# Two residuals taken one token tile at a time, and two matrix units whose last four weight chunks go token by token

## The chip, the cores and the metric

The kernel runs on one core of a Trainium2 chip. The metric is the device time of one execution in microseconds (us); lower is better. A core has five engines that run side by side, each through its own queue in order: PE (TensorE, matrix products and transposes), ACT (ScalarE), DVE (VectorE), POOL (GpSimd) and SP (here the issuer of most DMAs). Results of PE land in PSUM, from which ACT and DVE read.

## The reference, cut to what matters

The program is one layer of a hybrid decoder trunk: three token mixers, a merge, an MLP and a gated per-layer embedding, on 256 tokens of width 2048, in float32. The change touches the end of the mixer, the end of the MLP, and what follows each:

```python
mixed = jnp.sum(gates * up, axis=2) @ w_out[i]
x = x + rmsnorm(mixed, post_mix_norm[i])
h = rmsnorm(x, pre_mlp_norm[i])
m = jnp.square(jax.nn.relu(h @ w_up[i])) @ w_down[i]
x = x + rmsnorm(m, post_mlp_norm[i])
ple_gate = jax.nn.sigmoid(rmsnorm(x, ple_pre_norm[i]) @ w_ple_gate[i])
e = (p[i] @ w_ple_proj[i]) * ple_gate
x = x + rmsnorm(e, ple_post_norm[i])
```

`w_out` is 2048 x 2048, `w_up` 2048 x 8192, `w_down` 8192 x 2048, `w_ple_gate` 2048 x 2048, `w_ple_proj` 256 x 2048. The root mean square of a token runs over all 2048 columns, so a token's scale is known only when its last column block is.

## The kernel before

**Tiles.** The 256 tokens are two token tiles t = 0 and 1 of 128 partitions; the 2048 columns are four column blocks cb of 512, or 16 blocks k of 128. For the next product x must stand transposed (columns on partitions), as a pair hi and lo of rounded value and rest, `ahi` and `alo`, of 16 x 256 elements per partition (one buffer each).

**Weights.** `weights` (L289) brings a chunk of 2 x 128 rows by 512 columns: SP's DMA into `raw` (4 buffers), ACT's cast into `hi` (L302, 4 buffers), DVE's rest into `lo` (L303, recorded at L170, 4 buffers). A buffer comes free when PE has used its chunk, and the cast of the chunk four later waits for that.

**Products.** `gemm_tok` (L306) makes one unit of 512 columns for both token tiles: for each chunk 12 matmuls of 512 columns, three for each of two k and two tokens. In the last chunk (`held=1`) token 0's matmuls go ahead of token 1's; the rule is `elif kc + CK > nkt - held * CK: continue`, which gathers the steps of the last `held` chunks before they are sorted by token. The last unit of `w_ple_gate` already has `held=4`. `gemm_feat` (L333), used for `w_up`, has weights as the stationary side and both tokens side by side (256 columns), 24 matmuls for each chunk; so its first matmul needs k = 0 of both tokens.

**Seam 1**, between `w_out` and `w_up`: the last `w_out` unit's evac takes the sum of squares (`square_sum`, L1116, ACT, into `ssp`) and the product with the gain (`mx`, DVE). PE goes on with one small unit `proj_unit(0)` (12 matmuls of `w_ple_proj`; ACT copies it to `pj`). Meanwhile `residual` (L1146) makes the scale of both tokens at once (`rstd_of`, L1118: sum, scale, ACT square root L258, reciprocal L260, three small DVE steps), then, column block by column block, adds to x (`xr[t]`, called `b` in the trace; L1154, recorded at L173), transposes (PE, L123, into `br`, 4 banks) and splits (ACT L180 into `ahi`, DVE L173 into `alo`, 256 columns at a time). `stats` then squares the new x for the next norm, in ACT's free time.

**Seam 2**, between `w_down` and `w_ple_gate`, is the same with three `proj_unit`s (36 matmuls) behind the last `w_down` unit, and `gemm_tok` behind it, which takes the two tokens in turn, k by k. DVE also forms eight products `pg<-pj,b` there.

**Order.** A scheduler writes a fixed order for each engine, by priorities and its own costs; `residual` and the evacs stand under `tc.high_priority()`.

Of the kernel before, what the change touches and what calls it, by code (L numbers as in the profile page):

```python
# [12 lines left out]
ALU = mybir.AluOpType  # L13
AX = mybir.AxisListType

P = 128
# [36 lines left out]
def tile_hybrid_block(ctx: ExitStack, tc: tile.TileContext, *args):  # L53
# [118 lines left out]
    def stt(o, i0, s, i1, op0, op1):  # L172
        V.scalar_tensor_tensor(out=o, in0=i0, scalar=s, in1=i1, op0=op0, op1=op1)  # L173
# [132 lines left out]
    def gemm_tok(parts, act, nkt, evac, k0=0, held=1):  # L306


        n = sum(p[2] for p in parts)
        pb = [mbank() for _ in range(NT)]  # L310
        steps = []
        for kc in range(0, nkt, CK):
            hl = weights(parts, k0 + kc, CK, OFF_TOK)
            steps += [(kc, k, t, hl) for k in range(CK) for t in range(NT)]
            if kc + CK == nkt:
                steps.sort(key=lambda p: p[2])
            elif kc + CK > nkt - held * CK:
                continue
            for i, (kc_, k, t, (hi, lo)) in enumerate(steps):
                kt = kc_ + k  # L320
                xh, xl = act(kt, t)
                o = pb[t][:, :n]
                PE.matmul(o, lhsT=xh, rhs=hi[:, k, :n], start=(kt == 0), stop=False)
                PE.matmul(o, lhsT=xh, rhs=lo[:, k, :n], start=False, stop=False)
                PE.matmul(o, lhsT=xl, rhs=hi[:, k, :n], start=False, stop=(kt == nkt - 1))
                if i % 2:
                    background()
                if kt == nkt - 1:
                    with tc.high_priority():
                        evac(t, pb[t][:, :n])  # L330
            steps = []
# [786 lines left out]
    def rstd_of(parts):  # L1118
        n = parts.shape[1]
        s = sm(n)  # L1120
        V.tensor_reduce(out=s, in_=parts, axis=AX.X, op=ALU.add)
        return rstd(s, n, 1.0 / D)
# [10 lines left out]
    for cb in range(4):  # L1133
        def evac(t, pb, cb=cb):
            if cb == 0 and t == 0:
                phase_b()
            if t == 0:
                mg.append([tb("mx") for _ in range(NT)])
            if cb == 0:
                A.sqrt(out=sm(1), in_=r0[:, :1])  # L1140
            square_sum(pb, 512, ssp[:, t, cb:cb + 1])
            tt(V, mg[cb][t], pb, gains["g1"][:, cb * 512:(cb + 1) * 512], ALU.mult)
        gemm_tok([(w_out, cb * 512, 512)], macts, KT, evac)
    proj_unit(0)

    def residual(mg, parts, gcol):  # L1146

        hi, lo = actpair()
        with tc.high_priority():
            r = rstd_of(parts)  # L1150
            for cb in range(4):
                for t in range(NT):
                    xs = xr[t][:, cb * 512:(cb + 1) * 512]
                    stt(xs, mg[cb][t], r[:, t:t + 1], xs, ALU.mult, ALU.add)  # L1154
                for k in (0, 2):
                    transpose_into(lambda kt, t: xr[t][:, kt * P:(kt + 1) * P], (cb * 4 + k, cb * 4 + k + 1),
                                   hi, lo, cb * 4 + k, lambda kt: gainT[:, gcol + kt:gcol + kt + 1])
        out_r = const.tile([P, NT], F32, name=nm("rn"))

        def stats():  # L1160
            for t in range(NT):
                for cb in range(4):
                    square_sum(xr[t][:, cb * 512:(cb + 1) * 512], 512, ssn[:, t, cb:cb + 1])
                yield 1.0
            V.tensor_copy(out=out_r, in_=rstd_of(ssn))
        return acts(hi, lo), out_r, spawn(stats(), 6.0)
# [15 lines left out]
    for s in range(NSLAB):  # L1182
        hh = [mlp[0].tile([P, SK, S], F32R, tag=f"m{i}", bufs=1, name=nm(f"m{i}_")) for i in range(2)]
        for u in range(SLAB // 512):
            def evac(b, pb, u=u, hh=hh):
                z = t2()
                stt(r3(z, S), pb, 0.0, r2bc.unsqueeze(1).broadcast_to([P, 2, S]), ALU.max, ALU.mult)
                z2 = t2()
                tt(V, z2, z, z, ALU.mult)
                k = u * 4 + 2 * b  # L1190
                split_from(r3(z2, S), hh[0][:, k:k + 2, :], hh[1][:, k:k + 2, :])
            gemm_feat([(w_up, s * SLAB + u * 512, 512)], xact, KT, evac)
        mact = acts(*hh)
        for cb in range(4):
            def evac(t, pb, cb=cb, s=s):
                if s == 0:
                    A.copy(out=macc[cb][t], in_=pb)
                else:
                    tt(V, macc[cb][t], macc[cb][t], pb, ALU.add)
                if s == NSLAB - 1:  # L1200
                    square_sum(macc[cb][t], 512, ssp[:, t, cb:cb + 1])
                    tt(V, macc[cb][t], macc[cb][t], g3[:, cb * 512:(cb + 1) * 512], ALU.mult)
            gemm_tok([(w_down, cb * 512, 512)], mact, SK, evac, k0=s * SK)
    for cb in range(1, 4):
        proj_unit(cb)
    xact, r4, _ = residual(macc, ssp, 16)
# [67 lines left out]
```

## Time and profile before

| | |
|---|---|
| median of three runs | 1872.37 us (1867.6 to 1876.28) |
| the profiled execution | 1868.37 us |
| its span, first to last instruction | 1866.6 us |
| PE busy | 1829.7 us (98%) |
| DVE, ACT, POOL busy | 1160.5, 935.9, 184.2 us |
| mean granted TensorE clock | 0.992 |

The profile is one execution. All times below are us from the start of its span. A row of the timeline gives start, length, engine, line, operation, output and inputs, count, and in brackets the idle time of the engine before it with what ended it. Lengths overlap: a matmul of 512 columns lasts 0.39 us and the next starts about 0.227 us after it, so what a queue spends on an instruction is read from start to start.

### The profile page before, as it was taken

The page shows a single profiled execution, that of the slowest core. Times are in us where ns is not written, and L with a number is a line of the kernel's source. Part 1 is how long each engine was busy: PE and PEld are TensorE (multiplying, and loading weights), DVE is VectorE, ACT ScalarE, POOL GpSimd, SP SyncE. Part 2 cuts the span into 40 slices and gives each one's busy share as a digit, 9 for nine tenths or more (in the row PEclk, how much of TensorE's full clock was granted, in tenths as well). Part 3 has the DMA queues.
Part 4 walks back from the last instruction along what each step waited for, and adds up shares of the span by engine and source line. Part 5 has one row for each costly group of instructions (what it writes and reads, how often), then busy time and mean ns, then how long its engine had stood idle before and what let it go on. Part 6 is the DMA issues. An engine that isn't in the chain of part 4 may idle for free.

```text
span 1866.6 us, 28343 instructions
## 1 busy us (share of the span) xinstructions
PE 1829.7 (98%) x11256; PEld 1640.7 (88%) x11256; DVE 1160.5 (62%) x1518; ACT 935.9 (50%) x1200; POOL 184.2 (10%) x243
## 2 busy tenths in 40 slices
PE   8999999899999999999999999999999999999997
PEld 7999989899888788888888898899889988998886
DVE  6567847878567666554565765455555654565675
ACT  6745555576464565444444644444433433444654
POOL 0003814800201220000000000000000000000001
PEclk9999989999999999999999999999999999999999
DMA  7766556465665546666676566666666656666563
GB/s 251 217 188 181 143 165 190 125 191 145 205 203 169 170 139 193 196 184 192 191 243 204 187 194 193 193 192 183 192 193 189 188 195 193 183 190 192 180 211 128
DMA packets 185573, 348.07 MB, mean 186 GB/s; under 512 B 14296, under 2 KB 33103, under 8 KB 184544
## 3 DMA queue, kind: packets, MB, share of 16 engines
q1 hardware_dynamic: 182992, 334.69, 59.3%
q0 software_dynamic: 2416, 11.56, 1.9%
q8 instruction: 88, 1.44, 0.3%
q14 instruction: 45, 0.37, 0.1%
q10 hardware_dynamic: 32, 0.01, 0.0%
HBM read 340.41 MB, written 5.80 MB: 185 GB/s over the span
## 4 chain that ended last, share of the span: by engine, by line
PE 69%; ACT 1%; POOL 1%; DVE 1%; issue 0%; DVEq 0%; ACTq 0%
PE mm L114 67%; POOL b L170 1%; PE br L114 1%; PE br L123 1%; ACT hi L302 0%; DVE lo L170 0%; DVE b L173 0%; ACT b L947 0%; ACT b L948 0%; ACT L1228 0%; ACT b L1116 0%; ACT L1238 0%; ACT b L1226 0%; DVE s L173 0%; ACT b L941 0%
## 5 line engine op out<-in xcount | busy, mean ns | idle before, releaser
L170 DVE TENSOR_TENSOR lo<-raw,hi 128x1024 fp32r<-128x1024 f32 (+2 forms) x644 | 773.7, 1204 | 610.4 <-ACT hi L302 608.9
L302 ACT CAST hi<-raw 128x1024 fp32r<-128x1024 f32 (+2 forms) x644 | 654.1, 1019 | 793.2 <-PE mm L114 694.6
L114 PE MATMUL mm<-ahi,hi 128*128 128x256 f32 x1728 | 485.4, 281 | 0.0
L114 PE MATMUL mm<-alo,hi 128*128 128x256 f32 x1728 | 484.6, 281 | 0.7 <-DVE alo L173 0.7
L114 PE MATMUL mm<-ahi,lo 128*128 128x256 f32 x1728 | 484.5, 280 | 0.0
L114 PE MATMUL mm<-lo,ahi 128*128 128x512 f32 (+2 forms) x992 | 370.1, 373 | 3.2 <-DVE lo L170 2.1
L114 PE MATMUL mm<-hi,ahi 128*128 128x512 f32 (+2 forms) x992 | 372.9, 376 | 0.0
L114 PE MATMUL mm<-hi,alo 128*128 128x512 f32 (+2 forms) x992 | 368.4, 371 | 0.0
L114 PEld LDWEIGHTS mm<-ahi,lo 128*128 128x128 f32 x1728 | 329.0, 190 | 0.1
L114 PEld LDWEIGHTS mm<-alo,hi 128*128 128x128 f32 x1728 | 326.1, 189 | 1.7 <-DVE alo L173 0.9
L114 PEld LDWEIGHTS mm<-ahi,hi 128*128 128x128 f32 x1728 | 326.4, 189 | 0.6 <-ACT ahi L180 0.2
L114 PE MATMUL mm<-hi,m 128*128 128x512 f32 x1024 | 316.0, 389 | 0.0
L114 PEld LDWEIGHTS mm<-hi,m 128*128 128x128 f32 x1024 | 192.2, 188 | 39.8
L114 PEld LDWEIGHTS mm<-lo,ahi 128*128 128x128 f32 x992 | 187.7, 189 | 32.8 <-DVE lo L170 4.2
L114 PEld LDWEIGHTS mm<-hi,ahi 128*128 128x128 f32 x992 | 187.6, 189 | 28.2 <-issue 0.2
L114 PEld LDWEIGHTS mm<-hi,alo 128*128 128x128 f32 x992 | 187.7, 189 | 27.5
L114 PE MATMUL mm<-lo,m 128*128 128x512 f32 x512 | 199.3, 389 | 0.0
L114 PE MATMUL mm<-hi,b 128*128 128x512 f32 x416 | 134.1, 394 | 0.7 <-ACT hi L302 0.7
L114 PEld LDWEIGHTS mm<-lo,m 128*128 128x128 f32 x512 | 96.1, 188 | 19.8
L170 POOL TENSOR_TENSOR b<-b 128x128 f32<-128x128 f32 (+16 forms) x118 | 77.7, 673 | 160.1 <-ACT b L941 147.5
L114 PEld LDWEIGHTS mm<-hi,b 128*128 128x128 f32 x416 | 78.1, 188 | 17.0 <-ACT hi L302 1.1
L114 PE MATMUL mm<-lo,b 128*128 128x512 f32 x208 | 81.3, 391 | 0.8 <-DVE lo L170 0.8
(257 smaller groups left out, 1127.1 us busy)
## 6 DMA issues: line engine op xcount, KB each, us to landing
raw<-in_w_in_dram SPq DMA_DIRECT2D x200, 512.0 KB, 3.7
raw<-in_w_up_dram SPq DMA_DIRECT2D x128, 512.0 KB, 3.7
raw<-in_w_down_dram SPq DMA_DIRECT2D x128, 512.0 KB, 3.9
raw<-in_w_branch_dram SPq DMA_DIRECT2D x48, 512.0 KB, 4.5
raw<-in_w_in_dram SPq DMA_DIRECT2D x48, 344.0 KB, 3.6
raw<-in_w_out_dram SPq DMA_DIRECT2D x32, 512.0 KB, 4.9
raw<-in_w_ple_gate_dram SPq DMA_DIRECT2D x32, 512.0 KB, 4.7
raw<-in_w_in_dram SPq DMA_DIRECT2D x16, 352.0 KB, 3.2
```

The costliest lines, as they stand in the source:

```text
L114: nc.tensor.matmul(o, lhsT=lhsT, rhs=rhs, start=start, stop=stop, **kw)
L123: nc.tensor.transpose(o, i, ident)
L170: eng.tensor_tensor(out=o, in0=i0, in1=i1, op=op)
L302: A.copy(out=hi[:, :, :n], in_=raw[:, :, :n])
```

## The change

`residual` runs its outer loop over the two token tiles: each has its own scale (`rstd_of` on one column of sums), then for each column block the add, four transposes of 128 columns of that token into one bank, and four splits of 128 columns (where two tokens were split together, 256 columns). The last units of `w_out` and of `w_down` (fourth slab) get `held=4`: their last four chunks go first for token 0 (24 matmuls), then for token 1 (24).

```diff
-        gemm_tok([(w_out, cb * 512, 512)], macts, KT, evac)
+        gemm_tok([(w_out, cb * 512, 512)], macts, KT, evac, held=4 if cb == 3 else 1)
     proj_unit(0)
 
     def residual(mg, parts, gcol):
 
         hi, lo = actpair()
         with tc.high_priority():
-            r = rstd_of(parts)
-            for cb in range(4):
-                for t in range(NT):
+            for t in range(NT):
+                r = rstd_of(parts[:, t:t + 1, :])
+                sl = slice(t * P, (t + 1) * P)
+                for cb in range(4):
                     xs = xr[t][:, cb * 512:(cb + 1) * 512]
-                    stt(xs, mg[cb][t], r[:, t:t + 1], xs, ALU.mult, ALU.add)
-                for k in (0, 2):
-                    transpose_into(lambda kt, t: xr[t][:, kt * P:(kt + 1) * P], (cb * 4 + k, cb * 4 + k + 1),
-                                   hi, lo, cb * 4 + k, lambda kt: gainT[:, gcol + kt:gcol + kt + 1])
+                    stt(xs, mg[cb][t], r, xs, ALU.mult, ALU.add)
+                    pt = bank()
+                    for i in range(4):
+                        PE.transpose(pt[:, i * P:(i + 1) * P], xs[:, i * P:(i + 1) * P], ident)
+                    for i in range(4):
+                        k = cb * 4 + i
+                        split_from(pt[:, i * P:(i + 1) * P], hi[:, k, sl], lo[:, k, sl], gainT[:, gcol + k:gcol + k + 1])
...
-            gemm_tok([(w_down, cb * 512, 512)], mact, SK, evac, k0=s * SK)
+            gemm_tok([(w_down, cb * 512, 512)], mact, SK, evac, k0=s * SK,
+                     held=4 if s == NSLAB - 1 and cb == 3 else 1)
```

Instructions: ACT has 34 more (16 splits and one square root at each seam), DVE 44 more (16 splits and six steps of the scale at each seam); the transposes stay 32 at each seam, and SP's and POOL's orders are the same as before.

**Place 1: PE in seam 1.** Before; `b_1617`, `b_1618` are the operand of `w_ple_proj`, `b_1620` and `b_1621` are x of token 0 and 1, `cst` is the identity, `mm_10061` the first bank of `w_up`:

```order
L114 MATMUL mm_9931<-lo_9934,b_1617_9433 128x512
L114 MATMUL mm_9931<-hi_9933,b_1618_9434 128x512
L123 MATMUL br_9969<-cst,b_1620_9437 128x128
L123 MATMUL br_9978<-cst,b_1620_9437 128x128
L123 MATMUL br_9969<-cst,b_1621_9439 128x128
...
L123 MATMUL br_9989<-cst,b_1620_9437 128x128
L123 MATMUL br_9998<-cst,b_1620_9437 128x128
L114 MATMUL mm_10061<-ahi_9952,hi_10064 128x256
L114 MATMUL mm_10061<-ahi_9952,lo_10065 128x256
```

Of the change (`mm_10106` is now the first bank of `w_up`):

```order
L114 MATMUL mm_9931<-lo_9934,b_1617_9433 128x512
L123 MATMUL br_9968<-cst,b_1620_9437 128x128 x4
L114 MATMUL mm_9931<-hi_9933,b_1618_9434 128x512
L123 MATMUL br_9982<-cst,b_1620_9437 128x128 x4
L123 MATMUL br_9996<-cst,b_1620_9437 128x128 x4
L123 MATMUL br_10010<-cst,b_1620_9437 128x128 x4
L123 MATMUL br_10037<-cst,b_1621_9439 128x128 x4
L123 MATMUL br_10051<-cst,b_1621_9439 128x128 x4
L123 MATMUL br_10065<-cst,b_1621_9439 128x128 x4
L123 MATMUL br_10079<-cst,b_1621_9439 128x128 x4
L114 MATMUL mm_10106<-ahi_9952,hi_10109 128x256
```

Before, the first matmul of `w_up` stood behind ten transposes; now it stands behind all 32, the last 16 of which are of token 1.

**Place 2: DVE and ACT in seam 1.** DVE before, from the step that follows the last chunk's evac (`s_...` are the small steps of the scale, `mx_...` the products with the gain):

```order
L256 TENSOR_SCALAR s_1729_9956<-s_1728_9954 128x2
L170 TENSOR_TENSOR lo_10125<-raw_10123,hi_10124 128x1024
L260 RECIPROCAL s_1731_9960<-s_1730_9958 128x2
L170 TENSOR_TENSOR s_1732_9962<-s_1731_9960 128x2
L173 SCALAR_TENSOR_TENSOR s_1732_9962<-s_1732_9962,s_1729_9956 128x2
L173 SCALAR_TENSOR_TENSOR s_1733_9965<-s_1732_9962,s_1731_9960 128x2
L173 SCALAR_TENSOR_TENSOR b_1620_9437<-mx_9441,s_1733_9965,b_1620_9437 128x512
L173 SCALAR_TENSOR_TENSOR b_1621_9439<-mx_9442,s_1733_9965,b_1621_9439 128x512
```

DVE of the change, at the scale of token 0:

```order
L256 TENSOR_SCALAR s_1729_9956<-s_1728_9954 128x1
L170 TENSOR_TENSOR lo_9934<-raw_9932,hi_9933 128x1024
L260 RECIPROCAL s_1731_9960<-s_1730_9958 128x1
L170 TENSOR_TENSOR s_1732_9962<-s_1731_9960 128x1
L170 TENSOR_TENSOR lo_10110<-raw_10108,hi_10109 128x1024
L173 SCALAR_TENSOR_TENSOR s_1732_9962<-s_1732_9962,s_1729_9956 128x1
L173 SCALAR_TENSOR_TENSOR s_1733_9965<-s_1732_9962,s_1731_9960 128x1
L170 TENSOR_TENSOR lo_10140<-raw_10138,hi_10139 128x1024
L170 TENSOR_TENSOR mx_9897<-mm_9775,b_1619_9435 128x512
L173 SCALAR_TENSOR_TENSOR b_1620_9437<-mx_9441,s_1733_9965,b_1620_9437 128x512
```

ACT of the change, at the scale of token 1 (`s_1740`; the splits of token 0 above it begin with `br_9968` and go on in the same way, 16 in all):

```order
L1116 ACTIVATE b_1773_10190,ssn<-b_1620_9437 128x512
L180 ACTIVATE ahi_9952<-br_9968,rowT_493 128x128
L180 ACTIVATE ahi_9952<-br_9982,rowT_493 128x128
L180 ACTIVATE ahi_9952<-br_9996,rowT_493 128x128
L180 ACTIVATE ahi_9952<-br_10010,rowT_493 128x128
...
L258 ACTIVATE s_1740_10027<-s_1739_10025 128x1
L1116 ACTIVATE b_1774_10192,ssn<-b_1620_9437 128x512
L1116 ACTIVATE b_1775_10206,ssn<-b_1621_9439 128x512
L1116 ACTIVATE b_1776_10208,ssn<-b_1621_9439 128x512
L180 ACTIVATE ahi_9952<-br_10037,rowT_493 128x128
```

The adds of token 0 stand behind three weight rests and behind token 1's product `mx_9897`; the square root of token 1 stands behind all 16 splits of token 0.

**Place 3: PE and DVE in seam 2.** PE of the change, where token 1's transposes begin (`mm_16824` and `mm_16825` are the banks of the first `w_ple_gate` unit for token 0 and 1):

```order
L114 MATMUL mm_16824<-hi_16897,ahi_16678 128x512
L114 MATMUL mm_16824<-lo_16898,ahi_16678 128x512
L114 MATMUL mm_16824<-hi_16897,alo_16679 128x512
L123 MATMUL br_16763<-cst,b_1621_9439 128x128 x4
L123 MATMUL br_16777<-cst,b_1621_9439 128x128 x4
L114 MATMUL mm_16825<-hi_16827,ahi_16678 128x512
L123 MATMUL br_16791<-cst,b_1621_9439 128x128 x4
```

Before, the transposes of both tokens begin inside the last small unit (`mm_16612`) and end among the first `w_ple_gate` matmuls:

```order
L114 MATMUL mm_16612<-hi_16614,b_1617_9433 128x512
L123 MATMUL br_16650<-cst,b_1620_9437 128x128
L123 MATMUL br_16659<-cst,b_1620_9437 128x128
L114 MATMUL mm_16612<-lo_16615,b_1617_9433 128x512
L114 MATMUL mm_16612<-hi_16614,b_1618_9434 128x512
L123 MATMUL br_16650<-cst,b_1621_9439 128x128
```

DVE of the change, ahead of token 1's first add there:

```order
L260 RECIPROCAL s_2723_16755<-s_2722_16753 128x1
L170 TENSOR_TENSOR lo_16898<-raw_16896,hi_16897 128x1024
L173 SCALAR_TENSOR_TENSOR alo_16679<-br_16722,rowT_493,ahi_16678 128x128
L173 SCALAR_TENSOR_TENSOR alo_16679<-br_16736,rowT_493,ahi_16678 128x128
L170 TENSOR_TENSOR s_2724_16757<-s_2723_16755 128x1
L170 TENSOR_TENSOR pg<-pj_9928,b_2731_16819 128x512
...
L170 TENSOR_TENSOR pg<-pj_9929,b_2731_16819 128x512
L173 SCALAR_TENSOR_TENSOR s_2725_16760<-s_2724_16757,s_2723_16755 128x1
L170 TENSOR_TENSOR pg<-pj_16606,b_2731_16819 128x512
L173 SCALAR_TENSOR_TENSOR b_1621_9439<-mx_10097,s_2725_16760,b_1621_9439 128x512
```

Before, both tokens were through the scale together, ahead of any `pg` product; now token 1's scale is spread between weight rests, splits and `pg` products, and on PE its transposes follow 24 matmuls of token 0.

## Rows read from the trace of the kernel before

**Rows 1.** The page: busy time of the engines, share of the span, instructions.
```profile
PE 1829.7 (98%) x11256; PEld 1640.7 (88%) x11256; DVE 1160.5 (62%) x1518; ACT 935.9 (50%) x1200; POOL 184.2 (10%) x243
```
**Rows 2.** Timeline of PE around seam 1.
```profile
1038.66 0.39 PE L114 MATMUL mm<-hi,alo 128*128 128x512 f32 x1
1041.38 0.39 PE L114 MATMUL mm<-hi,b 128*128 128x512 f32 x1
1043.47 0.44 PE L123 MATMUL br<-cst,b 128*128 128x128 f32 x2 [1.70 <-DVE b L173]
1044.13 1.10 PE L123 MATMUL br<-cst,b 128*128 128x128 f32 x8 [0.22 <-DVE b L173]
1045.24 0.39 PE L114 MATMUL mm<-ahi,hi 128*128 128x256 f32 x1
...
1062.72 0.68 PE L114 MATMUL br<-cst,rb 128*128 128x128 f32 x4 [0.39 <-DVE rb L408]
1063.16 0.37 PE L114 MATMUL mm<-alo,hi 128*128 128x256 f32 x1
```
**Rows 3.** The chain that ended last, in order of time, in seam 1.
```profile
1053.47 5.59 PE mm L114 x49
1063.40 699.54 PE mm L114 x4514
```
**Rows 4.** Timeline of DVE in seam 1.
```profile
1042.27 0.36 DVE L173 SCALAR_TENSOR_TENSOR s<-s,s 128x2 f32<-128x2 f32 x2
1042.66 2.74 DVE L173 SCALAR_TENSOR_TENSOR b<-mx,s,b 128x512 f32<-128x512 f32 x4
1045.32 0.87 DVE L173 SCALAR_TENSOR_TENSOR alo<-br,rowT,ahi 128x256 fp32r<-128x256 f32 x2
...
1052.99 1.22 DVE L170 TENSOR_TENSOR lo<-raw,hi 128x1024 fp32r<-128x1024 f32 x1
```
**Rows 5.** Timeline of ACT in seam 1.
```profile
1039.67 1.04 ACT L302 CAST hi<-raw 128x1024 fp32r<-128x1024 f32 x1
1040.61 0.59 ACT L1111 COPY pj<-mm 128x512 f32<-128x512 f32 x1
...
1046.06 1.56 ACT L180 ACTIVATE ahi<-br,rowT 128x256 fp32r<-128x256 f32 x4
1047.48 0.66 ACT L1116 ACTIVATE b<-b 128x512 f32<-128x512 f32 x1
...
1052.30 0.64 ACT L1116 ACTIVATE b<-b 128x512 f32<-128x512 f32 x1
...
1052.91 0.64 ACT L1116 ACTIVATE b<-b 128x512 f32<-128x512 f32 x1
```
**Rows 6.** Groups by form: 128 columns from PSUM on ACT and DVE (busy us, mean ns).
```profile
L941 ACT COPY b<-br 128x128 f32<-128x128 f32 x8 | 2.0, 252 | 0.0
L170 DVE TENSOR_TENSOR cbm<-br,cst 128x128 f32<-128x128 f32 x4 | 1.1, 286 | 1.9 <-PE br L114 1.9
```
**Rows 7.** The timeline of PE: its longest idle stretch.
```profile
342.98 1.11 PE L123 MATMUL br<-cst,b 128*128 128x128 f32 x4 [6.04 <-ACT b L459]
```
**Rows 8.** Windows: length, busy PE, PEld, DVE, ACT, POOL (instructions), granted clock, DMA share, GB/s.
```profile
340.00:341.00 1.00, 0.00 (x0) 0.00 (x0) 1.00 (x2) 0.00 (x0) 0.92 (x2) 0.72 0.41 54
343.00:346.00 3.00, 3.00 (x14) 3.00 (x15) 1.89 (x5) 0.85 (x2) 2.77 (x4) 0.50 0.43 116
347.00:348.00 1.00, 1.00 (x10) 1.00 (x9) 0.83 (x1) 0.14 (x1) 0.92 (x2) 0.87 0.00 0
1041.50:1045.00 3.50, 1.58 (x12) 1.04 (x10) 3.36 (x9) 2.54 (x5) 0.00 (x0) 1.00 0.88 301
```
**Rows 9.** Timelines in seam 2: PE, and ACT behind the first unit.
```profile
1755.53 0.39 PE L114 MATMUL mm<-hi,m 128*128 128x512 f32 x1
...
1762.98 0.44 PE L123 MATMUL br<-cst,b 128*128 128x128 f32 x2
...
1790.36 1.06 ACT L302 CAST hi<-raw 128x1024 fp32r<-128x1024 f32 x1 [1.66 <-PE mm L114]
```

## The prediction, made before the changed kernel was run

> **What bounds the kernel now.** I read the page first. PE is busy 98% of the span, the next engine, DVE, 62% [rows 1]: nearly everything hides behind PE, and time is won or lost only where PE stands still. Next I read PE's timeline at the two seams that the change rewrites. In seam 1 PE ends the small unit with the matmul at 1041.38, then stands 1.70 and 0.22 us before transposes and 0.39 us before the row broadcast: 2.31 us in all [rows 2]. In seam 2, with 36 small matmuls as cover instead of 12, the transposes start at 1762.98 right behind the matmuls, and nothing is idle to speak of [rows 9]. In the chain of waits one unbroken stretch of PE, 699.54 us long, follows seam 1 [rows 3]: what seam 1 loses or gains is carried to the end. So the change can win some 2.3 us at most. What it can lose is as long as the new order makes PE wait, and that has to be followed queue by queue.
>
> **Prices, from start to start.** A 512-column matmul takes (1041.38 - 1038.66)/12 = 0.227 us [rows 2], a 256-column one 5.59/49 = 0.114 [rows 3]. DVE: a 512-column add 2.66/4 = 0.665, a 256-column split (0.87 - 0.08)/2 = 0.395, a weight rest 1.22 - 0.08 = 1.14 (the last 0.08 of each overlap the next, as the add shows: 0.74 for the last of four that take 2.66 from start to start), a small step 0.39/2 = 0.19 [rows 4]. ACT: a cast 0.94, a copy `pj` 0.49 (0.59 long, less the cast's overlap of 0.10), a 256-column split 1.42/4 = 0.355, a square with its read 0.61 [rows 5]. A group of four transposes takes about 0.46 (eight take 1.10 to the end of the last) [rows 2].
>
> The new 128-column split does not occur. It cannot cost less than half of the wide one (0.18 on ACT, 0.20 on DVE) nor more than the whole (0.355, 0.395), since each pair of new splits does one old one's columns. The nearest rows are 128 columns from PSUM at 252 ns on ACT and 286 ns on DVE [rows 6]; against the 512-column copy's 0.59 us [rows 5] that is about 0.9 ns for a column on ACT, and against the add's 0.74 us about 1.2 ns on DVE. So I take off 128 columns at 0.9 and 1.0 ns: 0.25 on ACT, 0.26 on DVE. A gain is excluded here: the columns are the same and the instructions twice as many. The Trainium skill (page "ScalarE: Activation LUTs", section "What ACT_TABLE_LOAD costs") gives an ACTIVATE 186 ns + 0.833 ns a column, 93 ns more for a pointer operand, 93 ns of overlap: an estimate of 0.29 us for 128 columns. By that page the seam 1 sum below would be some 0.4 us longer; for 256 columns it would say 0.40, where this trace shows 0.355, so the trace's slope stands.
>
> **Held chunks, alone.** The same 48 matmuls run in another order. The fourth held chunk's cast waits for the chunk before the four, as now, and is ready some 2.4 us into token 0's pass, where its first matmul comes 18 x 0.227 = 4.1 us in: no wait. The cost is later: held buffers come free only during token 1's pass, after its 6th, 12th, 18th and 24th matmul.
>
> **Seam 1, step by step, on the clock of the trace of before.** The last `w_out` matmul starts at 1038.66 as before [rows 2], so token 0 is finished 24 matmuls earlier, at 1038.66 + 0.39 - 5.44 = 1033.6.
>
> *Head start of token 0.* Its sum of squares and square root could be through by about 1036.2. But on DVE three weight rests and token 1's product stand between (place 2). Their casts wait for the buffers freed at 1035.0, 1036.3 and 1037.7; each is followed by 1.14 us on DVE, with the small steps in between: the rests start at 1036.1, 1037.6 and 1039.1, token 1's product at 1040.3, and the first add of token 0 at 1040.9, the fourth at 1042.9 (end 1043.6). Before, the first add was at 1042.66 [rows 4]. A head start of 5.4 us has become 1.8.
>
> *PE.* The small unit hides the adds up to 1041.4; the four groups of token 0 follow the adds and end at 1044.1. Next in PE's queue is token 1's first group, and no matmul of `w_up` stands ahead of it (place 1).
>
> *Scale of token 1.* Its square root is queued on ACT behind all of token 0's splits (place 2). ACT first squares token 0's two new blocks as their adds end (1041.6, 1042.3) and is through the second `pj` copy at 1043.4; then 16 splits x 0.25 + a cast 0.94 + a square 0.61 = 5.55: the root at about 1049.0. DVE, with a weight rest first and then the lo splits at 0.26 behind ACT's, is through at 1049.55. Then reciprocal 0.19, one more weight rest 1.14, three small steps 0.57: the first add of token 1 at 1051.45, its end at 1052.2. PE stands from 1044.1 to 1052.26: 8.1 us, where before it stood 1.9.
>
> *The clock.* PE's one idle stretch of this length in the trace is 6.04 us, from 336.94 to 342.98 [rows 7]. The granted clock was at its upper level (2.4 GHz) until some way into 340 to 341 (mean 0.72, so until 340.4), at its lower (0.50, 1.2 GHz) from 343 to 346, and up again in 347 to 348 (mean 0.87, so from 347.3), 4.3 us after PE took up work [rows 8]. The 1.70 us stand in seam 1 left it at 1.00 [rows 8]. So here the clock is down when token 1's groups come, and each takes 2 x 0.46: 1052.26 + 3.7 = 1055.95. If it is up again 4.3 us after 1052.26, the first 0.6 us of `w_up` runs at half pace (0.3 lost). Splits of token 1 keep ahead of `w_up` from there: k = 0 is split by 1054.6, k = 3 by 1057.7, and 24 matmuls of a chunk take 2.74.
>
> *Sum.* Before, 125 matmuls of `w_up` and the row broadcast (0.44 from 1062.72) were done when the matmul at 1063.16 started, with 22 of the transposes between them [rows 2]. Now: 1055.95 + 0.3 + 125 x 0.114 + 0.44 = 1070.9. Loss **+7.8 us**. Were the clock to hold, the groups would end at 1054.7 and the loss would be +6.2. Were it up again only 4.3 us after `w_up` begins, 2.1 instead of 0.3 would be lost there: +9.6. Splits at their upper bound add 1.6, at their lower bound take off 0.7 (ACT's root is then not the last to come; DVE's rests are).
>
> **Seam 2.** 36 small matmuls cover more. The last `w_down` matmul starts at 1755.53 [rows 9], so the held buffers come free at 1751.8, 1753.2 and 1754.6; three casts and rests bring DVE to 1757.2, token 1's sum to 1757.8, and token 0's adds start at 1757.8, 1758.4, 1760.0 and 1761.1, with a product and splits between. PE waits only 0.3 for the first group. PE then has the rest of the small units and 24 matmuls of `w_ple_gate` for token 0 and comes to token 1's transposes at 1771.5 (place 3). ACT has one copy, two squares, three splits' worth and a cast until 1761.5, then ten splits, four copies, a square and a cast up to token 1's root: 10 x 0.25 + 4 x 0.49 + 0.61 + 0.94 = 6.0, root at 1767.5. DVE reaches the reciprocal at 1768.6, behind two weight rests; then a rest 1.14, three splits 0.78, three `pg` products (priced as the add, 0.665) and small steps that tuck in at 0.08: first add at 1772.9, end 1773.6. PE waits 2.1. Later it meets matmuls of the fifth `w_ple_gate` chunk, whose cast stands behind 11 splits and three squares on ACT (cast at 1777.7) and whose rest ends at 1780.0: waits of 0.9 and 0.5. By the end of the unit's 96 matmuls (before: 1790.3, the release that the cast at 1790.36 waited for [rows 9]) I get 1793.9. Loss **+3.6 us**. This is the softer number: every wait is short against the sums it comes from; I bound it by 1.0 (the first and last waits gone, the middle one halved) and 5.5 (each sum 10% longer).
>
> **Total.** +7.8 + 3.6 = +11.4 us. Against the profiled execution: 1868.37 + 11.4 = 1879.8 (span 1878.0, and 1.8 around it). That execution lay 4.0 below the median of the three runs, so for a median I predict 1872.37 + 11.4 = **1883.8 us**. A measurement of this kernel can tell about 0.5% from no change, that is 9.4 us: the forecast is slower by 0.6%, only just outside.
>
> **Rivals.**
> *Small loss, no measurable change* (chance 0.28): seam 1 as above with the clock held (+6.2), and seam 2 near its lower bound (+1.0 to +3): +7.2 to +9.2, 1880 to 1881.5. For it: seam 2 has the long cover, and in seam 1 the transposes resume little by little. Against it: PE stands longer than in the stretch where the clock did fall.
> *Larger loss* (0.13): the clock comes back late in seam 1 (+9.6) and falls in seam 2 as well, where PE stands 2.1 us and soon twice more (about +2 on 3.6): +15.2, 1887.6. For it: the return after 4.3 us is a single observation, and PE resumes here in four pieces that wait for DVE. Against it: the stand of 1.70 left the clock alone.
> *The head start works* (0.04), the other side: token 0's adds, transposes and splits run under token 1's pass, only token 1's path remains, and PE's 2.31 us of idle in seam 1 go: 1870.1. Place: DVE's queue. It decides for this if the adds of token 0 start before about 1036.5, so that their 16 splits end with token 1's matmuls; they would start at 1040.9, since three weight rests stand ahead and wait for buffers that the held chunks keep. I find nothing for it in the orders.
> That the change doesn't do what it says is excluded by the orders shown.
>
> **How the numbers follow.** Forecast (+9.4 to +13.5) 0.55, small loss 0.28, larger 0.13, head start 0.04. The range takes in the small and the larger loss (+7.2 to +15.2) and 3.5 us on either side, since medians of three move too (the three runs span 8.7): low 1872.37 + 3.7 = 1876, high 1872.37 + 18.7 = 1891; it leaves out the head start. Slower by over 0.5%: most of the forecast, all of the larger loss, 0.65; within 0.5%: the small loss and the forecast's edge, 0.33; faster 0.02.
>
> **What would show it.** Right: PE's wait for DVE's adds at L173 (now 1.9 us, 2 times) grows to about 8 in seam 1 and 2 more in seam 2; the granted clock falls to 0.5 for some 8 us near 1048 and is back before 1060; the square root of token 1 in seam 1 lies some 5.5 us behind ACT's first narrow split; narrow splits on ACT come 0.25 apart. Wrong: `w_up` begins before 1050 (the head start works, or the narrow splits are far cheaper); the clock stays at 1.00 (then +9.9 in all); seam 2 shows no wait at its second token (then about +8).

## The result, and the profile after

The changed kernel takes 1883.21 us (median; 1881.14 to 1887.27) against 1868.52 us of before, run beside it: a ratio of 1.0068, 95% interval 1.0048 to 1.0088, slower by 0.7%. The prediction was 1883.8 us and slower. The medians lie 14.7 us apart, the ratio stands for 12.7, and the five executions of before span 8.7, so it is in part luck that the forecast of the median was met within 0.6 us. The profiled execution of the changed kernel took 1881.42 us, with a span of 1879.6 us, 13.0 us more than that of before.

The sum came out, the parts less so. To see them, every trace is read in the same way: the start of a matmul is counted from the start of the last `w_out` matmul (1038.66 in [rows 2], 1038.62 after), so that what differs ahead of the change drops out. Three marks on PE then cut the difference from before: PE's 183rd instruction after that matmul (needless ones of the experiments not counted; for e7 twelve more, which it moves ahead; it lies behind the row broadcast in all traces but e9's), at the end of `w_up`'s first slab, and at the last matmul of all.

| | seam 1, to the 183rd instruction | rest of the first `w_up` slab | later `w_up` slabs | seam 2 | sum |
|---|---|---|---|---|---|
| predicted | +7.8 | 0 | 0 | +3.6 | +11.4 |
| measured | +6.5 | +2.8 | 0.0 | +3.2 | +12.6 |

PE's timeline in seam 1, the changed kernel; it answers to [rows 2]:

```profile
1041.41 0.66 PE L123 MATMUL br<-cst,b 128*128 128x128 f32 x4
1042.14 1.98 PE L123 MATMUL br<-cst,b 128*128 128x128 f32 x12
1051.83 3.29 PE L123 MATMUL br<-cst,b 128*128 128x128 f32 x16 [7.71 <-DVE b L173]
1054.88 0.37 PE L114 MATMUL mm<-ahi,hi 128*128 128x256 f32 x1
...
1065.86 0.61 PE L114 MATMUL br<-cst,rb 128*128 128x128 f32 x4
```

Where PE stood 1.70 and 0.22 us, it now stands 7.71 (the total below takes in seam 2's 1.78). The row broadcast no longer waits. PE's waits, the whole span (total, times, longest):

```profile
PE br L123 <- DVE b L173: 9.5, 2, 7.7
```

What PE waits for stands on ACT and DVE. ACT in seam 1, from token 0's second half on (it answers to [rows 5]):

```profile
1046.11 0.68 ACT L1116 ACTIVATE b<-b 128x512 f32<-128x512 f32 x1
1046.63 0.26 ACT L1116 ACTIVATION_READ_ACCUMULATOR b<-b 128x1 f32 x1
1046.72 2.22 ACT L180 ACTIVATE ahi<-br,rowT 128x128 fp32r<-128x128 f32 x8
1048.71 0.32 ACT L258 ACTIVATE s<-s 128x1 f32<-128x1 f32 x1
```

Token 1's square root is the last row: it came when the sixteenth split of token 0 was done, 10.1 us after the last `w_out` matmul (before: 2.4). DVE beside it (answers to [rows 4]):

```profile
1038.88 1.23 DVE L170 TENSOR_TENSOR lo<-raw,hi 128x1024 fp32r<-128x1024 f32 x1
1040.02 0.68 DVE L170 TENSOR_TENSOR mx<-mm,b 128x512 f32<-128x512 f32 x1
1040.62 2.73 DVE L173 SCALAR_TENSOR_TENSOR b<-mx,s,b 128x512 f32<-128x512 f32 x4
...
1044.47 2.19 DVE L173 SCALAR_TENSOR_TENSOR alo<-br,rowT,ahi 128x128 fp32r<-128x128 f32 x8
...
1047.17 2.16 DVE L173 SCALAR_TENSOR_TENSOR alo<-br,rowT,ahi 128x128 fp32r<-128x128 f32 x8 [0.45 <-ACT ahi L180]
1049.25 0.15 DVE L260 RECIPROCAL s<-s 128x1 f32<-128x1 f32 x1
1049.32 1.21 DVE L170 TENSOR_TENSOR lo<-raw,hi 128x1024 fp32r<-128x1024 f32 x1
...
1051.02 2.74 DVE L173 SCALAR_TENSOR_TENSOR b<-mx,s,b 128x512 f32<-128x512 f32 x4
```

Token 0's adds start at 1040.62, right behind the third weight rest and token 1's product; token 1's adds at 1051.02, behind all splits of token 0, a reciprocal, another rest and the small steps. The granted clock of the same stretch (windows; columns: width, busy time of PE, PEld, DVE, ACT and POOL with counts, clock, DMA share, GB/s; answers to [rows 8]):

```profile
1046.00:1047.00 1.00, 0.00 (x0) 0.00 (x0) 0.72 (x4) 1.00 (x6) 0.00 (x0) 1.00 0.92 360
1047.00:1048.00 1.00, 0.00 (x0) 0.00 (x0) 0.83 (x4) 1.00 (x6) 0.00 (x0) 0.89 0.85 336
1048.00:1051.00 3.00, 0.00 (x0) 0.00 (x0) 2.92 (x11) 1.64 (x7) 0.00 (x0) 0.50 0.14 55
1051.00:1054.00 3.00, 2.17 (x10) 2.17 (x11) 2.98 (x5) 2.19 (x7) 0.00 (x0) 0.50 0.58 175
1054.00:1055.00 1.00, 1.00 (x9) 1.00 (x8) 0.62 (x3) 1.00 (x5) 0.00 (x0) 0.70 0.00 0
1055.00:1060.00 5.00, 5.00 (x47) 5.00 (x46) 4.52 (x18) 4.63 (x17) 0.00 (x0) 1.00 0.01 3
```

It fell at about 1047.8 and was back at about 1054.6, some 2.8 us after PE took up work. PE in seam 2 (answers to [rows 9], which has no idle time):

```profile
1782.61 1.32 PE L123 MATMUL br<-cst,b 128*128 128x128 f32 x8 [1.78 <-DVE b L173]
...
1787.69 0.77 PE L114 MATMUL mm<-hi,ahi 128*128 128x512 f32 x2 [0.57 <-ACT hi L302]
1788.95 0.50 PE L114 MATMUL mm<-lo,ahi 128*128 128x512 f32 x1 [0.25 <-DVE lo L170]
```

**A term that was not in the sum.** PE does not wait in the rest of the first `w_up` slab, neither before nor after, and yet the changed kernel loses 2.8 us there. One of PE's three groups of `w_up` matmuls from 1080 to 1120, before (count; busy time, mean ns of one; idle time):

```profile
L114 PE MATMUL mm<-ahi,lo 128*128 128x256 f32 x119 | 32.9, 276 | 0.0
```

The same group in the changed kernel:

```profile
L114 PE MATMUL mm<-ahi,lo 128*128 128x256 f32 x114 | 32.1, 281 | 0.0
```

With the other two groups that is 355 matmuls before and 342 after in the same 40 us, the two or three that only reach into the window counted in. From start to start it is one every 0.1133 or every 0.1178 us (the pace; 272 or 283 cycles at the granted 2.4 GHz). Over some 630 matmuls of the slab that makes 2.8 us. In the changed kernel the matmuls run at 0.1133 up to the row broadcast and at 0.1178 from there to the end of the slab. Slabs 2 to 4 run at 0.1178 in both kernels.

### The profile page after: what moved, and what is told of

It is laid out like the page before. It is cut to its first block, busy times and chain, and to the rows that moved or that the text cites. A ratio compares the mean times of both kernels' runs of the same rounds, so it can differ in the third digit from the quotient of the medians.

```text
span 1879.6 us, 28418 instructions
## 1 busy us (share of the span) xinstructions
PE 1835.1 (98%) x11256; PEld 1645.5 (88%) x11256; DVE 1167.2 (62%) x1562; ACT 940.3 (50%) x1234; POOL 183.0 (10%) x243
## 4 chain that ended last, share of the span: by engine, by line
PE 68%; ACT 2%; DVE 1%; POOL 1%; issue 1%; DVEq 0%; ACTq 0%
PE mm L114 66%; POOL b L170 1%; PE br L114 1%; PE br L123 1%; ACT hi L302 1%; DVE lo L170 1%; ACT b L1116 0%; ACT ahi L180 0%; DVE b L173 0%; ACT pj L1111 0%; ACT b L947 0%; ACT b L948 0%; DVE alo L173 0%; DVE pg L170 0%; DVE pj L170 0%
```

## The experiments

The theory from the prediction, S: the order inside the new residual costs, above all the root of token 1 behind token 0's splits. The rival, H: the held chunks cost, since they bring three weight rests ahead of the adds. Later ones are told where they came up. Differences below are of the traces, from the last `w_out` matmul; ratios are of times, against before beside it. Each kernel has one trace. How far such a difference repeats is seen where the order of seam 1 is the same: the order of the changed kernel stands in e3 and e12 as well, and the three lose 6.5, 6.9 and 6.7 us there; the order of before stands in e11 and e6 as well, which lose 0.0 and, with a fall of the clock (see e9), 1.3.

**e1: held chunks alone.**

```diff
-        gemm_tok([(w_out, cb * 512, 512)], macts, KT, evac)
+        gemm_tok([(w_out, cb * 512, 512)], macts, KT, evac, held=4 if cb == 3 else 1)
...
-            gemm_tok([(w_down, cb * 512, 512)], mact, SK, evac, k0=s * SK)
+            gemm_tok([(w_down, cb * 512, 512)], mact, SK, evac, k0=s * SK,
+                     held=4 if s == NSLAB - 1 and cb == 3 else 1)
```

> Only the held chunks of the change (both units), with the residual of before, both tokens' scale at once. Theory S (the order inside the new residual costs: token 1's square root stands on ACT behind token 0's sixteen splits): the seams stay within 2 us of before, because nothing new stands ahead of the roots; 1868 to 1871 us, ratio 1.000 to 1.002, PE's wait at the adds stays near 2 us and the granted clock stays at 1.00 there. Rival H (the held chunks cost: they keep weight buffers, so three weight rests come late and stand on DVE ahead of the adds): most of the loss is here already, 1876 us or more.

Ratio 1.0007 (0.9992 to 1.0021). Seam 1 -0.07 us, all else 0.00: the three rests do come late, but they end just as token 1's sum is due. H falls.

**e2: the new residual alone** (the diff of the change without the two `held` lines).

> Only the new residual, one token tile at a time, without held chunks. Theory S: nearly the whole loss of the change, since the head start of token 0 was never worth much: PE stands 6 to 8 us for token 1's adds in seam 1, the clock falls there, 1878 to 1883 us, ratio 1.005 to 1.008. Rival H: within 3 us of before, up to 1872 us. If the slower pitch of the first w_up slab's matmuls in the changed kernel (0.118 us from start to start against 0.113) belongs to the new residual, it is here too.

Ratio 1.0053 (1.0033 to 1.0073). Seam 1 +7.4, first slab +2.8, seam 2 +3.8: 14.0 us, more than the whole change. By the traces the held chunks win back 0.9 and 0.5 us of what the new residual loses, and S stands so far. (That e2 loses more than the change is not shown by the times: +14.0 would be a ratio of 1.0075, just above e2's interval, and e2's ratio lies below the 1.0068 of the change. It rests on one trace of each, and the 0.9 is not far above the 0.4 by which seam 1 of one and the same order differs.)

**e3: the change at seam 1 alone** (`residual` takes its old body for the second seam, `w_down` no held chunks).

> Both parts of the change at the first seam (w_out to w_up), the second seam as before. By the trace of the change 6.5 us of the loss lie in the seam itself, 2.9 us in the first w_up slab behind it, whose matmuls start 0.118 us apart instead of 0.113, and 3.2 us in seam 2. So if the pitch comes with the seam: 1868.5 + 9.4 = 1877.9 us. If the pitch is a matter of the single execution: between 1875 and 1878 and the first slab may start its matmuls 0.113 apart. Rival: seam 2 costs more than the trace shows, then 1873 or less here.

Ratio 1.0040 (1.0025 to 1.0056). Seam 1 +6.9, first slab 0.0, the rest 0.0. The seams are independent, and the slab's pitch is not tied to the seam's new order: here the first `w_up` matmuls ran at 0.1178, and from the row broadcast on at 0.1133. The same PE group in e3, 1080 to 1120:

```profile
L114 PE MATMUL mm<-ahi,lo 128*128 128x256 f32 x118 | 32.6, 276 | 0.0
```

**e4: both scales ahead of the loop over tokens.**

```diff
-            for t in range(NT):
-                r = rstd_of(parts[:, t:t + 1, :])
+            rs = [rstd_of(parts[:, t:t + 1, :]) for t in range(NT)]
+            for t in range(NT):
+                r = rs[t]
```

> The whole change, but both tokens' scales are written ahead of the loop over tokens, so that ACT takes token 1's square root ahead of token 0's splits (in its order behind the cast, the first copy and one square). Theory S: token 1's root comes at about 1042.3 instead of 1048.7, its first add at about 1046.3, PE stands 2 to 3 us instead of 7.7, too short for the clock to fall; the loss falls to between +0 and +4: 1868 to 1873 us. Rival H: the loss stays, 1877 us or more, because the rests ahead of token 0's adds stay where they are.

Ratio 1.0052 (1.0035 to 1.0069). The root moved as wanted, from 10.1 to 3.5 us after the last `w_out` matmul (which starts at 1041.52 here), but seam 1 still loses 4.1, the first slab 2.8 and seam 2 2.0: the expected 0 to 4 us in all were missed, and PE stands 4.2 us instead of the expected 2 to 3. ACT's root in e4's timeline:

```profile
1044.98 0.19 ACT L258 ACTIVATE s<-s 128x1 f32<-128x1 f32 x1
```

DVE behind it, the rest and token 1's first add:

```profile
1047.08 1.21 DVE L170 TENSOR_TENSOR lo<-raw,hi 128x1024 fp32r<-128x1024 f32 x1
...
1049.25 0.73 DVE L173 SCALAR_TENSOR_TENSOR b<-mx,s,b 128x512 f32<-128x512 f32 x1
```

PE, with its longest wait:

```profile
1051.73 2.29 PE L123 MATMUL br<-cst,b 128*128 128x128 f32 x8 [4.19 <-DVE alo L173]
```

Between the root and token 1's first add at 1049.25 (7.7 us after the last `w_out` matmul; before it was the second of the four adds from 1042.66, so 4.7) DVE still does adds and splits of token 0 and a weight rest. That add ends at 1049.98, and PE still does not start: its wait of 4.2 us ends with a split on DVE, so its last 1.7 us are for a bank that token 0's splits have not yet emptied. Here too the clock fell, at 1051.8, for 3.4 us. S as first put is too narrow: moving the root won 2.5 of the 6.5 us; behind it stands DVE's queue.

**e8: held chunks and a scale for each token, but column block by column block, with the wide splits of before.** The diff is against the kernel before; the two `held` lines of e1 go with it.

```diff
-            r = rstd_of(parts)
+            r = [rstd_of(parts[:, t:t + 1, :]) for t in range(NT)]
             for cb in range(4):
                 for t in range(NT):
                     xs = xr[t][:, cb * 512:(cb + 1) * 512]
-                    stt(xs, mg[cb][t], r[:, t:t + 1], xs, ALU.mult, ALU.add)
+                    stt(xs, mg[cb][t], r[t], xs, ALU.mult, ALU.add)
```

> Held chunks on both units and a scale for each token, both scales written first, but then column block by column block with both tokens and the wide splits of before: the head start without the token by token order. Theory S2 (after e4: w_up's first matmul needs the first columns of both tokens, and the token order puts token 0's sixteen splits and the four banks ahead of them): the loss is gone, within 1.5 us of before at seam 1 and seam 2, PE's longest wait at most 3 us, 1867 to 1872 us. Rival (the second scale itself costs, a second chain of six small steps and a root across two engines): 3 us or more are lost in seam 1.

Ratio 1.0032 (1.0015 to 1.0048): seam 1 +3.5, first slab +2.8, seam 2 +0.9. The rival held, not S2: the second scale alone, by which e8 differs from e1, costs 3.5 us where e1 costs nothing. DVE's timeline in seam 1 of e8 (the last `w_out` matmul starts at 1045.45, ACT's root at 1048.92):

```profile
1049.56 0.16 DVE L260 RECIPROCAL s<-s 128x1 f32<-128x1 f32 x1
1049.63 0.73 DVE L173 SCALAR_TENSOR_TENSOR b<-mx,s,b 128x512 f32<-128x512 f32 x1
1050.28 0.15 DVE L170 TENSOR_TENSOR s<-s 128x1 f32<-128x1 f32 x1
1050.35 1.22 DVE L170 TENSOR_TENSOR lo<-raw,hi 128x1024 fp32r<-128x1024 f32 x1
1051.49 0.15 DVE L173 SCALAR_TENSOR_TENSOR s<-s,s 128x1 f32<-128x1 f32 x1
1051.56 1.22 DVE L170 TENSOR_TENSOR lo<-raw,hi 128x1024 fp32r<-128x1024 f32 x1
1052.69 0.15 DVE L173 SCALAR_TENSOR_TENSOR s<-s,s 128x1 f32<-128x1 f32 x1
1052.88 2.74 DVE L173 SCALAR_TENSOR_TENSOR b<-mx,s,b 128x512 f32<-128x512 f32 x4
```

PE there:

```profile
1053.69 2.82 PE L123 MATMUL br<-cst,b 128*128 128x128 f32 x12 [4.21 <-DVE b L173]
```

Small steps of 0.15 us that depend on one another have an add and two weight rests put between them: token 1's first add comes 7.4 us after the last `w_out` matmul instead of 4.7. These 2.8 us are most of the loss of 3.5; the clock was at 0.50 from 1053.3 to 1056.7, while the twelve transposes ran, and how much of the other 0.7 that is, is not separated.

**e9: narrow splits alone**, in the kernel before (cut; `w` is 128 in both residuals).

```diff
-                split_from(pt[:, i * S:(i + 1) * S], hi[:, kd + i, :], lo[:, kd + i, :], gain(kt))
+                for o in range(0, S, w):
+                    split_from(pt[:, i * S + o:i * S + o + w], hi[:, kd + i, o:o + w], lo[:, kd + i, o:o + w], gain(kt))
```

> The kernel before, where the splits of both residuals alone are cut from 256 to 128 columns; order, scales and chunks are as before. By the changed kernel's trace a narrow split spends 0.25 us on ACT and 0.27 on DVE, so a pair costs 0.15 more on each engine than one wide one. Theory (the splits are a small part of the loss; they run behind w_up's matmuls once those have begun): 0.3 to 1.5 us in seam 1, since four pairs stand ahead of the first w_up matmuls, nothing in seam 2: 1869 to 1872 us, ratio 1.000 to 1.001. Rival (the doubled count of splits is the loss): 4 us or more.

Ratio 1.0012 (0.9999 to 1.0025): seam 1 +2.0, first slab (where its row broadcast falls) +0.5, seam 2 +0.1. The rival falls. It is more than expected in seam 1, and the clock fell there as well, about when stands of 1.71, 0.22 and 0.23 us were over; before, stands of 1.70 and 0.22 left it alone. One row of e9's windows:

```profile
1050.00:1053.00 3.00, 3.00 (x14) 3.00 (x15) 2.20 (x7) 2.54 (x11) 0.00 (x0) 0.50 0.41 151
```

What such a fall is worth can be read from e6 (below), which changes nothing in seam 1: PE, ACT and DVE have the order of before there, and PE's stands are the same, but the clock fell for 3.4 us. PE and one row of the windows of e6:

```profile
1047.40 0.44 PE L123 MATMUL br<-cst,b 128*128 128x128 f32 x2 [1.71 <-DVE b L173]
1048.06 1.63 PE L123 MATMUL br<-cst,b 128*128 128x128 f32 x8 [0.22 <-DVE b L173]
1049.00:1051.00 2.00, 2.00 (x12) 2.00 (x11) 1.91 (x5) 1.59 (x5) 0.00 (x0) 0.50 0.66 256
```

The eight transposes took 1.10 before and take 1.63 here, and seam 1 loses 1.3 us by the clock alone. Taken off e9's 2.5 us of seam 1 and first slab, it leaves an estimated 1.2 for the narrow splits and for the pace of 0.1178 at which e9's `w_up` matmuls ran up to the row broadcast: within what was expected.

**e5 and e10: work for PE while it stands**, in the changed kernel. e10's edit (e5 had 52 transposes and a bank of the `br` pool):

```diff
             for t in range(NT):
+                if t and gcol == 0:
+                    pt = mbank()
+                    for i in range(66):
+                        PE.transpose(pt[:, i % 4 * P:(i % 4 + 1) * P], xs[:, :P], ident)
                 r = rstd_of(parts[:, t:t + 1, :])
```

> The changed kernel with 52 needless transposes on PE in seam 1, between the groups of token 0 and those of token 1, into a bank of their own that nothing reads: PE works where it stood 7.7 us, so the granted clock should stay at 1.00. It tells what the half clock costs. Theory A (token 1's groups follow DVE's adds, 0.68 us apart, so the half clock hardly shows): w_up begins 0.5 to 0.7 us earlier than in the changed kernel, 1882 to 1883 us. Theory B, that of the prediction (a group takes 0.92 us at half pace against 0.46, and the clock costs the four groups 1.85 us): w_up begins 1.5 to 2 us earlier, 1881 us. If the clock falls all the same, the fillers don't stand where PE waits, and nothing is told.

> As e5, with 66 needless transposes into a bank of the other pool, so that they can start right behind token 0's last group and PE works on until token 1's adds come; in PE's order the last two groups of token 1 now stand among the first w_up matmuls. The granted clock should hold at 1.00 through seam 1. Theory A (the groups follow the adds): from the last w_out matmul to the row broadcast 0.3 to 1.0 us less than in the changed kernel. Theory B (the half clock costs the four groups 1.85 us): 1.5 to 2.5 less. If it holds and nothing is won, the clock's fall cost nothing here.

e5 (ratio 1.0084, 1.0055 to 1.0113; seam 1 +10.0) tells nothing on the price of the clock: its transposes waited 4.50 us for a bank, and the clock fell at 1045.8. In e10 PE is busy and the clock holds (windows):

```profile
1048.00:1051.00 3.00, 3.00 (x30) 3.00 (x28) 2.94 (x10) 3.00 (x10) 0.00 (x0) 1.00 0.77 294
1051.00:1054.00 3.00, 3.00 (x30) 3.00 (x29) 2.61 (x10) 2.86 (x13) 0.00 (x0) 1.00 0.65 255
```

Seam 1 loses 5.5 instead of 6.5 us: by these two traces the half clock cost 1.0 us, the top of theory A, with two reserves: two groups of token 1 have moved behind the first `w_up` matmuls here, and the times (ratio 1.0072, 1.0051 to 1.0093) cannot tell 1 us.

**e6, e11, e12: the pitch of the slabs.** e11 on the kernel before (e12 the same on the changed one, in the first slab too):

```diff
         for kc in range(0, nkt, CK):
+            if kc == CK and tick:
+                pt = bank()
+                for i in range(tick):
+                    PE.matmul(pt[:, i * P:(i + 1) * P], lhsT=ident, rhs=ident, start=True, stop=True)
...
-            gemm_feat([(w_up, s * SLAB + u * 512, 512)], xact, KT, evac)
+            gemm_feat([(w_up, s * SLAB + u * 512, 512)], xact, KT, evac,
+                      tick=2 if s and u == 0 else 0)
```

> The kernel before, with w_up's slabs 2 to 4 disturbed. In both kernels their matmuls of 256 columns start 0.118 us apart all through, while the first slab of before runs at 0.113 and that of the changed kernel at 0.118 from the row broadcast on. Slab 2: two needless fp32 matmuls of 128 columns, as in the row broadcast, behind the first chunk and without a wait. Slab 3: two needless transposes ahead of the first matmul that wait for the evac of w_down's last bank (about 1.2 us). Slab 4: one needless fp32 matmul behind the first chunk. Theory T (the pitch is a state that an interruption by 128-column matmuls switches and that then holds): the slabs that switch gain 720 x 0.0045 = 3.2 us each, less 0.2 to 1.2 for the disturbance: 1860 to 1863 us if all three switch, ratio 0.995 to 0.997. Rival W (the pitch comes with the weights' or the activations' addresses, or with the chunk's supply): all three stay at 0.118, 1870.5 us.

> The kernel before with the disturbance that e6 showed to be the cheapest, two needless fp32 matmuls of 128 columns behind the first chunk, in each of w_up's slabs 2 to 4. Theory T (the pitch of a slab is a state that this interruption switches from 0.118 to 0.113): each of the three slabs gains 2.85 us as slab 2 did in e6, 8.5 us in all, ratio 0.9954, 1863 us. Rival (slab 2 of e6 switched by chance): some slabs stay at 0.118 and the gain is 0 to 6 us.

> The changed kernel with the same disturbance in its four w_up slabs, in the first one at the second unit. Theory T: the first slab, at 0.118 since the row broadcast, goes to 0.113 from the second unit on and wins back some 2 of the 2.8 us that lie between the seams; with the other three slabs 10.5 us less in all: 1872.5 us, and the loss against e11 falls from 14.7 to about 12. Rival (the slow pitch of the first slab comes with the token order, as where ahi and alo are read): the first slab stays at 0.118.

e6: ratio 0.9971 (0.9955 to 0.9987). Slab 2, behind two needless fp32 matmuls, went to 0.1133 and won 2.85 us, the disturbance paid; slab 3 went to 0.1133 too (3.3 won, 1.2 paid for the interruption ahead of it); slab 4 stayed at 0.1178. But slab 4 was not disturbed: its one fp32 matmul waits for nothing, and in PE's order it came ahead of slab 3 (its two rows at 1403.09), with the two waiting transposes behind it:

```profile
1403.09 0.39 PE L114 MATMUL br<-cst 128*128 128x128 f32 x2
1404.12 0.44 PE L123 MATMUL mm<-cst,mx 128*128 128x128 f32 x2 [0.65 <-DVE mx L170]
1404.31 0.36 PE L114 MATMUL mm<-ahi,hi 128*128 128x256 f32 x1
```

So e6 does not tell whether slab 3 switched by the wait or by the single matmul, nor what a single matmul does inside a slab. Seam 1 of e6 lost 1.3 us (see e9). e11: ratio 0.9959 (0.9944 to 0.9974), and -2.85 us in each of the three slabs. The interruption in slab 2, in PE's timeline of e11:

```profile
1233.16 0.61 PE L114 MATMUL br<-cst 128*128 128x128 f32 x4
1233.52 0.37 PE L114 MATMUL mm<-ahi,hi 128*128 128x256 f32 x1
```

The PE group of slab 2 in e11, 1260 to 1300:

```profile
L114 PE MATMUL mm<-ahi,lo 128*128 128x256 f32 x118 | 32.6, 276 | 0.0
```

And in before, the same 40 us:

```profile
L114 PE MATMUL mm<-ahi,lo 128*128 128x256 f32 x114 | 32.0, 281 | 0.0
```

e12: ratio 1.0004 (0.9990 to 1.0018). All four slabs switched; the first won back 2.0 us, the others 2.85 each. So the 2.8 us of the first slab are not work that the change added but a state that set in at its row broadcast; e3, with the same order up to there, came out of it in the other state. e11 is faster than both kernels, by 0.41% (0.26 to 0.56) against before.

**e7: cover instead of a head start**, in the kernel before.

```diff
     proj_unit(0)
+    proj_unit(1)
...
-    for cb in range(1, 4):
+    for cb in range(2, 4):
         proj_unit(cb)
```

> The kernel before, with its four small units of w_ple_proj two and two: 24 matmuls behind w_out instead of 12, and 24 behind w_down instead of 36. It asks what the change aimed at in another way: PE's 2.3 us of idle time in seam 1. Theory: 2.7 us more of cover hide the stands of 1.70 and 0.22 us in seam 1, the 0.39 before the row broadcast stays, and in seam 2 the 5.4 us that are left still cover the 4.9 us from the last matmul to the first transposes as seam 1 shows them: 1.5 to 2 us less, ratio 0.999. Rival: DVE's eight pg products and ACT's copies make seam 2 longer than seam 1, and PE stands there instead: no gain.

Ratio 0.9999 (0.9981 to 1.0016): the rival. Seam 1's stands at the transposes are gone (the one at the row broadcast grows from 0.39 to 1.22), but PE now stands as long in seam 2, and the clock falls there at 1769.4 for 3.4 us. With the twelve moved matmuls (2.7 us) counted to either side, the trace wins 0.9 us in seam 1 and loses 3.1 in seam 2; the times cannot tell these 2.3 us from nothing. The timeline of e7:

```profile
1768.23 0.44 PE L123 MATMUL br<-cst,b 128*128 128x128 f32 x2 [1.61 <-DVE b L173]
1768.89 1.51 PE L123 MATMUL br<-cst,b 128*128 128x128 f32 x8 [0.22 <-DVE b L173]
```

## Why the prediction came out, step by step

*Held chunks, alone: nothing.* Right (e1). That they free buffers late was seen rightly too; it hurts no one while both tokens share a scale.

*Prices.* A narrow split was put at 0.25 us on ACT and 0.26 on DVE. Eight in a row take 2.22 on ACT and 2.16 on DVE; with 0.35 and 0.34 for the last one (as long as the single ones at 1053.16 and 1053.68) that is (2.22 - 0.35)/7 = 0.27 and (2.16 - 0.34)/7 = 0.26. By the figures of the Trainium skill (page "ScalarE: Activation LUTs", section "What ACT_TABLE_LOAD costs") the estimate for ACT is 0.29 for 128 columns; the trace's 0.27 lies between it and the prediction's price.

*Head start, 1.8 us.* Right: token 0's first add was put at 1040.9 and came at 1040.62.

*Scale of token 1.* Right in place and size: root 1049.0 against 1048.71, first add 1051.45 against 1051.02, PE's stand 8.1 against 7.71. As a cause it was told too simply. e4 and e8 show three causes one behind the other: the root on ACT (2.5 us of the 6.5), DVE's adds, splits and rests between root and add, and the banks; the shares of the last two are not separated.

*The clock.* That it falls was right; the price was not. The prediction let the four groups run at 0.92 us each (3.7) and put the return 4.3 us after PE's start. They took 3.05, without idle time in between: at half clock the transposes started 0.21 us apart, 0.85 for a group, and the clock was back after 2.8, so that the last three ran 0.11 apart. `w_up` began at 1054.88 instead of 1055.95. The prediction's sums with and without the fall (+7.8 and +6.2) price it at 1.6 us, e10 at 1.0; even at full clock the last group cannot start before DVE's fourth add ends, at 1053.76. This is the mis-sized term of seam 1: +7.8 predicted, +6.5 measured.

*The matmuls behind the seam.* The failed step. The sum took 0.114 us for every `w_up` matmul from one stretch [rows 3] and carried seam 1's loss unchanged to the end. The same matmuls have two paces, and the changed kernel ran the slab at the slower: +2.8.

*Seam 2.* +3.6 against +3.2; the waits of 2.1, 0.9 and 0.5 measured 1.78, 0.57 and 0.25, the clock stayed at 1.00.

So the total was hit within 1.2 us with errors of -1.3, +2.8 and -0.4, which partly cancel: that is luck. Without the slab's pace the loss would have been 9.8 us, on the edge of the 0.5% that the prediction named.

## What to carry to other kernels

A step on a shared scale that is split in two doubles a chain of tiny dependent instructions, and on an engine with a fixed order each link can catch a long neighbour: look at what stands between the links, not at the links. A head start is worth what the next in-order queue leaves of it. When PE shows no wait and still falls behind, compare the start-to-start time of the same matmuls in both traces before looking for a cause in the change.

## What the runs showed of the hardware

**Two paces of one matmul stream.** 256-column fp32r matmuls with a new weight load each start 0.1133 or 0.1178 us apart at a granted clock of 1.00, and keep the pace for hundreds of instructions. Two needless fp32 matmuls of 128 columns switched 0.1178 to 0.1133 in 8 of 8 slabs (e6, e11, e12). A row broadcast for which PE had waited was followed by 0.1133 in all six traces that have one (before, e1, e6, e7, e9, e11), but only in e9 did the stream run at 0.1178 ahead of it. One without a wait went from 0.1133 to 0.1178 in six traces (after, e2, e4, e8, e10, e12), the other way in e3, and left 0.1178 as it was in e5. Slabs that follow 512-column matmuls directly began at 0.1178 each time. The needless matmuls show in the trace as four rows of 128 columns, as the row broadcast does, and were only tried at 0.1178; what they do to a slab at 0.1133 is not shown. What the state is stays open. The Trainium skill (page "TensorE: Matmul & The Clock Gate", section "Back-to-back issue gap") gives N/2.4 + 2.5 ns for the gap of an isolated matmul, 109 ns for 256 columns; both measured paces lie above it.

**The clock is no clean function of the stands.** In one and the same order of instructions, stands of 1.70 or 1.71 and 0.22 us left it at 1.00 before and in e11, and were followed by 3.4 us at 0.50 in e6, which cost 1.3 us. It held in e1 as well, and fell behind 1.71, 0.22 and 0.23 us in e9 and behind 1.61 and 0.22 us in seam 2 of e7.

**Executions differ ahead of the change.** The last `w_out` matmul starts between 1033.7 and 1045.8 in these traces, from differences between about 240 and 480 us. Counting from it made effects of 1 us and more readable in single profiles, where times of whole executions scatter by more; one order of seam 1 still differs by 0.4 us between traces (after, e3, e12), and by 1.3 where the clock fell in one and held in the other (e6, before).
